# Sixteen weight sums of a two-layer decoder step, moved from the second half's attention to the first half's shared keys and heads

## The chip, the cores and the metric

The kernel runs on one core of a Trainium2 chip. The metric is the device time of one execution in microseconds (us), from the runs of one program on the chip; lower is better. All tensors are fp32. A product of two fp32 matrices is made of three TensorE products of split operands (high times high, high times low, low times high), so that each weight tile is loaded, rounded into a high part by ScalarE, and its rest taken by VectorE, before TensorE can use it.

## The reference, cut to what matters

The reference is one step of a two-layer decoder for a prompt of 1024 tokens and 8 sample tokens, model width 1024, feed-forward width 2816 (22 blocks of 128).

```python
# layer 0: h = h + norm(mixer_a(norm(h)));  h = h + norm(swiglu(norm(h), w_gu[0], w_down[0]))
sb_k, sb_v = split(rmsnorm(h, g_kv) @ w_kv)          # shared keys and values, once, after layer 0
# layer 1: mixer_b(norm(h)) = [stick_breaking(q_s, sb_k, sb_v), mem_attend(q_m, mem_k, mem_v)] @ w_o[1]
#          h = h + norm(mix);  h = h + norm(swiglu(norm(h), w_gu[1], w_down[1]))
def swiglu(h, w_gu, w_down):
    gate, up = split(h @ w_gu, 2)
    return (silu(gate) * up) @ w_down
```

The sample tokens attend, in layer 1, over 256 past tokens each, whose keys and values lie in pages (`cache_sb_k`, `cache_sb_v`) that `page_table` names, and over 256 memory tokens each (`cache_mem_k`, `cache_mem_v`).

## The kernel before, in words

**Two halves.** The prompt is worked in two halves of 512 tokens, g = 0 and g = 1; the 8 sample tokens ride with g = 1, which so has 520 columns. Everything is held transposed: feature blocks of 128 on the partitions, tokens along the free dimension. Each half goes through layer 0 and layer 1. Generators (`a0`, `a1`, `b0`, `b1` for the mixers, `f0`, `f1`, `fw` for the feed-forward, `o0`, `o1` for the output projections) yield after small pieces, and `weave` interleaves several generators in given proportions. The instruction order of every engine is fixed when the program is built; what `weave` decides is the order written into each engine's queue.

**The body's order around the change** (lines 1512 to 1547): `f0` ends layer 0 of g = 0. Then come `o1.mm` (output projection of layer 0 for g = 1, line 400, whose copy out of PSUM is line 388 in `evac_raw`) beside `f0.finish` and `normed`; `kv_proj(0)` (line 1251: four key heads through `proj`, whose copy to SBUF is line 1271, and the values through `rows_proj`, matmul line 1018); `normed` for layer 1; `b0.heads()` (eight heads of queries through `heads2`, copy line 1202) beside `o1.finish()`. `o1.finish` begins with `residual` (line 355): it loads four tiles `ht` of the input (line 362), turns them on TensorE (line 370) and adds them to the projection on VectorE (lines 371 and 373). Then comes `b0`'s attention beside `f1`'s first two parts, `fw`'s three parts, and the same sequence for the other half, up to `b1`'s attention (line 1542). That last stage holds `b1.sb` and `b1.mem` for the prompt, `b1.sb_sample` and `b1.mem_sample` for the sample tokens, and four parts of `f0`'s feed-forward.

**Weights.** `split_w` (line 194) loads 256 KB of weights as 512-byte rows into one of 5 raw tiles `w` (line 199, SyncE's queue), ScalarE rounds it (line 204), VectorE takes the rest (line 205), into one of 5 tiles `ws`. `rows_proj` does the same with rows of 2 KB (lines 1010 to 1013). All plain loads and stores are issued by SyncE (SP) in one order.

**The sample's attention.** `sample_scores` (line 893) loads for each of the 8 tokens its keys `c` (pages through GpSimd, line 953; memory through SP, line 941) and its query, spread over the partitions, `b<-qd` (line 911), multiplies them on VectorE (line 912) and reduces them. `sample_pv` (line 918) loads the values, multiplies (line 924) and adds (line 925) on VectorE, and collects them in a matmul `ns` (line 926). The tiles `c` come from a pool of 4. VectorE takes these instructions in the order of its queue, between the weight rests and the prompt's attention.

**Weight sums.** Part of the feed-forward for g = 1 (`gate_up_w`, line 471) uses seven products of half size instead of eight, and needs sums of blocks of `w_gu` for that. `weight_sums(l, parts)` (line 538) makes them by DMA alone, in DRAM tiles `wsum`: for each part eight steps, four that copy (line 556) and four that add into the destination (line 554).

```python
mark = nc.gpsimd.tensor_copy(small([P, 1], tag="mk", bufs=1), now[0])   # line 551
with tc.issue_after(mark.ins):
    if add: nc.gpsimd.dma_start(d, a, accum_op=ALU.add)                 # line 554
    else:   nc.gpsimd.dma_start(d, a, max_dma_last_dim=4 * w)           # line 556
```

The mark is a copy of one column of `now[0]`, the tile that the other work wrote last when the step was recorded; so GpSimd (POOL) reaches the step's DMA only once that tile is written. Steps of one part depend on each other (step 3 adds into what step 1 copied, step 4 into what step 2 copied, and steps 5 to 8 follow each other), and POOL waits for the landing of the step before. The parts of the feed-forward are 5, 5, 4, 4 and 4 blocks; a step of the first two parts has 1280 KB, of the others 1024 KB.

`ws` is the generator of layer 1's forty steps (parts 0 to 4). Before, steps 1 to 16 (parts 0 and 1) run beside `b0`'s attention, steps 17 to 24 (part 2) beside `fw`, and steps 25 to 40 (parts 3 and 4) beside `b1`'s attention. All are read in the last stage, `f1 = ffn_w(1, ...)`.

Of the kernel before, what the change touches and what calls it, by code (L numbers as in the profile page):

```python
# [23 lines left out]
def tile_decoder(  # L24
# [8 lines left out]
    ND = D // P  # L33
# [57 lines left out]
    def N():  # L91
        return npool.tile([P, WID], F32, tag="n", name=nm("n"))
# [14 lines left out]
    def X(g):  # L107
        return xpool.tile([P, 2, NG[g]], F32R, tag=f"x{g}", name=nm("x"))
# [42 lines left out]
    def gcol(l, i, k):  # L151
        o = (l * 4 + i) * ND + k
        return par[:, o : o + 1]
# [13 lines left out]
    def drain(*gens):  # L167
        for g_ in gens:
            for _ in g_:
                pass  # L170

    def chain(*gens):
        for g_ in gens:
            yield from g_

    def weave(*streams):

        live = [[0, n, g_] for g_, n in streams]
        while live:
            cur = min(live, key=lambda e: e[0] / e[1])  # L180
            cur[0] += 1
            try:
                next(cur[2])
            except StopIteration:
                live.remove(cur)
# [5 lines left out]
    def sv(ap, g):  # L191
        return ap[:, :G] if g == 0 else ap.rearrange("p (a n) -> p a n", a=2)
# [31 lines left out]
    def split_to(dst, src):  # L224
        nc.scalar.copy(dst[0], src)  # L225
        nc.vector.tensor_sub(dst[1], src, dst[0].bitcast(F32))  # L226
# [25 lines left out]
    def sq_acc(acc, src, k, n):  # L252
        if k == 0:
            nc.scalar.activation(acc[:, :n], src, AF.Square)
        else:
            t = N()
            nc.scalar.activation(t[:, :n], src, AF.Square)  # L257
            nc.vector.tensor_add(acc[:, :n], acc[:, :n], t[:, :n])  # L258

    def normed(g, R, rstd, gc, out, keep=False):  # L260
        n = NG[g]
        for k in range(ND):
            t = N() if keep else R[k]
            nc.vector.scalar_tensor_tensor(t[:, :n], R[k][:, :n], gc(k), rstd[:, :n], op0=ALU.mult, op1=ALU.mult)
            x = X(g)
            split_to((x[:, 0, :n], x[:, 1, :n]), t[:, :n])
            out.append(x)
            yield
# [43 lines left out]
        nc.vector.tensor_scalar(xt, xt, ss[:n], None, op0=ALU.mult)  # L312

    made = [None]

    def start(g, out):
        if g:
# [66 lines left out]
    def evac_raw(g, R, ps, m, acc, first, last):  # L384
        n = NG[g]
        dst = sv(R[m], g)
        if first:
            nc.scalar.copy(dst, pv(ps, g))
        else:
            nc.vector.tensor_add(dst, dst, pv(ps, g))  # L390
        if last:
            sq_acc(acc, R[m][:, :n], m, n)

    class out_proj:

# [130 lines left out]
        now[0] = mt[:, 0, 0:1].bitcast(F32)  # L526
        return mt

    now = [None]
    act = [None]  # L530
    sums = {}

# [5 lines left out]
    def weight_sums(l, parts):  # L538

        for i in parts:  # L540
            f0, nf = PARTS[i]
            w = nf * P
            s1, s2, s3, s4 = (tc.dram_tile([512, w], F32, name=nm("wsum")) for _ in range(4))
            sums.setdefault(l, {})[i] = (s1, s2, s3, s4)
            a11, a12 = (w_gu[l][r : r + 512, f0 * P : f0 * P + w] for r in (0, 512))
            a21, a22 = (w_gu[l][r : r + 512, DFF + f0 * P : DFF + f0 * P + w] for r in (0, 512))
            for d, a, add in (
                (s3, a11, False), (s1, a21, False), (s3, a21, True), (s1, a22, True),
                (s2, s3, False), (s2, a22, True), (s4, s2, False), (s4, a12, True),
            ):  # L550
                mark = nc.gpsimd.tensor_copy(small([P, 1], tag="mk", bufs=1), now[0])
                with tc.issue_after(mark.ins):
                    if add:
                        nc.gpsimd.dma_start(d, a, accum_op=ALU.add)
                    else:
                        nc.gpsimd.dma_start(d, a, max_dma_last_dim=4 * w)
                yield
# [122 lines left out]
    class ffn:  # L680
# [4 lines left out]
        def part(self, pi):  # L685
            g, l = self.g, self.l
            n = NG[g]
            f0, nf = PARTS[pi]
            last = pi == len(PARTS) - 1
            mids = []  # L690
            for j in range(nf):
                pg = proj(g, w_gu[l], 0, ND, (f0 + j) * P, self.xt)
                sg = silu(None, pg, g)
                pu = proj(g, w_gu[l], 0, ND, DFF + (f0 + j) * P, self.xt)
                nc.vector.tensor_mul(sv(sg, g), sv(sg, g), pv(pu, g))  # L695
                mt = M(F32R)
                split_to((mt[:, 0, :n], mt[:, 1, :n]), sg[:, :n])
                mids.append(mt)
                now[0] = mt[:, 0, 0:1].bitcast(F32)
                yield  # L700
            if pi == 0:
                self.R = R_one()
            if last:
                self.acc = small([P, WID], tag="st", bufs=3)
            for m in range(ND):
                ps = proj(g, w_down[l], f0, nf, m * P, mids)
                evac_raw(g, self.R, ps, m, self.acc, pi == 0, last)
                now[0] = self.R[m][:, 0:1]
                if m % 2:
                    yield  # L710

# [539 lines left out]
    def kv_proj(g, xt):  # L1251
        ks = small([P, 2, H, NB], tag="ks", bufs=1) if g else None
        for j, (out, scr) in enumerate(((sbk_prompt, ksc), (sbv_prompt, vsc))):
            if j and not g:
                rows = [C(), C()]
                yield from rows_proj(w_kv, H * P, xt, rows)
                for i in range(2):
                    t0 = 2 * i * P
                    nc.sync.dma_start(
                        out[0, t0 : t0 + 2 * P].rearrange("(c p) h d -> p c (h d)", p=P), rows[i]  # L1260
                    )
                    for h in range(H):
                        nc.sync.dma_start(
                            scr[h][:, g, t0 : t0 + 2 * P].rearrange("p (c d) -> p c d", c=2),
                            rows[i][:, :, h * P : (h + 1) * P],
                        )
                continue
            for h in range(H):
                ps = proj(g, w_kv, 0, ND, (j * H + h) * P, xt)
                t = T()  # L1270
                nc.scalar.copy(sv(t, g), pv(ps, g))
                if g:
                    nc.vector.tensor_copy(ks[:, j, h, :], t[:, G : G + NB])
                pt = S()
                for c in range(CH):
                    nc.tensor.transpose(pt[:, c * P : (c + 1) * P], t[:, c * P : (c + 1) * P], ident)
                tok = T()
                nc.vector.tensor_copy(tok[:, :G], pt)
                nc.sync.dma_start(
                    out[0, g * G : (g + 1) * G, h, :].rearrange("(c p) d -> p c d", p=P),  # L1280
                    tok[:, :G].rearrange("p (c d) -> p c d", d=P),
                )
                nc.sync.dma_start(scr[h][:, g, :], t[:, :G] if j == 0 else tok[:, :G])
                yield
        if g:
            for j, dst in enumerate((sbk_sample, sbv_sample)):
                pt = S()
                for h in range(H):
                    nc.tensor.transpose(pt[:NB, h * P : (h + 1) * P], ks[:, j, h, :], ident)
                t = T()  # L1290
                nc.vector.tensor_copy(t[:NB, :512], pt[:NB, :])
                nc.sync.dma_start(dst.rearrange("b o h d -> (b o) (h d)"), t[:NB, :512])
            yield
# [139 lines left out]
    with tc.issue_after(made[0].ins):  # L1433
# [16 lines left out]
        for lv in range(7):  # L1450
            m = 1 << lv
# [48 lines left out]
    a1 = mixer_a(1, x1)  # L1500
# [6 lines left out]
    f0 = ffn(0, 0, o0.x)  # L1507
# [5 lines left out]
    xk0, xb0 = [], []  # L1513
    o1 = out_proj(1, 0, M)
    drain(o1.mm(a1.xo, 0, 1))
    weave((f0.finish(True), 9), (o1.mm(a1.xo, 1, 5), 4))
    weave((normed(0, f0.R, f0.r, gkvcol, xk0, True), 8), (o1.mm(a1.xo, 5, 7), 2))
    drain(kv_proj(0, xk0))
    weave((normed(0, f0.R, f0.r, lambda k: gcol(1, 0, k), xb0), 8), (o1.mm(a1.xo, 7, ND), 1))
    b0 = mixer_b(0, xb0)  # L1520
    weave((b0.heads(), 8), (o1.finish(), 17))
    b0.open()
    f1 = ffn(1, 0, o1.x)
    ws = weight_sums(1, range(5))
    weave((chain(b0.sb(), b0.mem()), 25), (chain(f1.part(0), f1.part(1)), 18), (islice(ws, 16), 17))
    set_banks(True)
    fw = ffn_w(0, o1.x, (5, 6, 5), 2, False, f1.R)
# [13 lines left out]
    f0 = ffn(0, 1, o0.x)  # L1541
    weave(
        (chain(b1.sb(), b1.mem()), 45), (chain(b1.sb_sample(), b1.mem_sample()), 39),
        (chain(f0.part(0), f0.part(1), f0.part(2), f0.part(3)), 34), (ws, 17),
    )
    o1 = out_proj(1, 1, A, True)
    drain(o1.mm(b1.xo))
# [37 lines left out]
```

## Time and profile before

| | before |
|---|---|
| median of 3 runs | 2512.58 us (2512.22 to 2516.48) |
| the profiled execution's own time | 2513.78 us |
| its span, first to last instruction | 2511.9 us |
| mean granted TensorE clock | 0.995 |
| TensorE matmul busy | 2467.7 us |
| VectorE busy | 1609.2 us |
| ScalarE busy | 1197.4 us |
| GpSimd busy | 119.6 us |

The profile is of one execution. Engines are named PE (TensorE matmul), PEld (its weight load), DVE (VectorE), ACT (ScalarE), POOL (GpSimd) and SP (SyncE, which issues DMAs). A row of the timeline or of the chain begins with its start in us from the span's start and its length in us; in square brackets stands how long the engine was idle before it and who ended that. A row of the stretches view gives for one stretch of time its length, each engine's busy time with the number of instructions, the granted TensorE clock (1.00 is full speed), the busy share of the 16 DMA engines and the rate in GB/s. In the DMA view, q1 is the queue that SP fills and q0 the one that POOL fills; the last column of a queue's row is the share of the 16 engines' time that its packets took, and the last number of an issue row is the median time from issue to landing.

### The profile page before, as it was taken

What the parts mean: (1) busy time and instruction counts of PE and PEld (TensorE: products, weight loads), DVE (VectorE), ACT (ScalarE), POOL (GpSimd) and SP (SyncE); (2) the same over time, 40 slices, a digit from 0 to 9 for tenths busy, and PEclk for the clock granted to TensorE, in tenths of its full rate; (3) what the DMA queues carried; (4) which work ended last, traced back from release to release, by engine and by line L of the source; (5) the groups of instructions that cost most, each with busy time, mean ns of one, the idle gap of its engine ahead of it and who ended that gap; (6) DMA issues with size and microseconds to landing.
All of it is one profiled execution on the core that took longest, in us unless ns stands there. A gap on an engine that the chain in (4) does not pass through costs nothing.

```text
span 2511.9 us, 40889 instructions
## 1 busy us (share of the span) xinstructions
PE 2467.7 (98%) x15455; PEld 2160.5 (86%) x15455; DVE 1609.2 (64%) x2900; ACT 1197.4 (48%) x2289; POOL 119.6 (5%) x187
## 2 busy tenths in 40 slices
PE   8999999999999999999999999999999999999998
PEld 6888888877877898999999989876677798999998
DVE  5766556654766576665655676776687538845666
ACT  5437543243433454554434554554454335554445
POOL 1000000000000000010100100021000000000000
PEclk9999999999999999999999999999999999999999
DMA  5355656554743447476767746575456643464552
GB/s 189 116 158 126 162 174 164 130 145 144 195 122 101 130 138 219 148 181 163 187 177 194 221 139 191 167 193 143 135 167 169 167 123 118 134 186 140 150 151 73
DMA packets 521550, 391.24 MB, mean 156 GB/s; under 512 B 19973, under 2 KB 459858, under 8 KB 521354
## 3 DMA queue, kind: packets, MB, share of 16 engines
q1 hardware_dynamic: 493194, 308.94, 41.4%
q0 software_dynamic: 28160, 79.70, 13.4%
q8 instruction: 121, 1.98, 0.3%
q14 instruction: 75, 0.61, 0.1%
HBM read 358.76 MB, written 101.11 MB: 183 GB/s over the span
## 4 chain that ended last, share of the span: by engine, by line
PE 90%; DVE 4%; DMA 3%; ACT 1%; issue 1%; SPq 0%; POOL 0%; DVEq 0%; ACTq 0%
PE mm L218 53%; PE q L499 11%; PE q L631 7%; PE q L453 2%; PE s L1150 2%; PE mm L1018 2%; DMA b<-qd 1%; PE s L1343 1%; PE s L885 1%; PE s L854 1%; PE mm L803 1%; PE mm L830 1%; PE s L1314 1%; PE q L663 1%; PE ns L926 1%
## 5 line engine op out<-in xcount | busy, mean ns | idle before, releaser
L218 PE MATMUL mm<-x,ws 128*128 128x512 f32 (+1 forms) x6624 | 1216.0, 340 | 2.4 <-DVE t L235 1.5
L218 PEld LDWEIGHTS mm<-x,ws 128*128 128x128 f32 x6624 | 1013.6, 189 | 155.5 <-issue 17.4
L204 ACT CAST ws<-w 128x512 fp32r<-128x512 f32 (+1 forms) x672 | 395.1, 589 | 616.8 <-PE mm L218 468.3
L205 DVE TENSOR_TENSOR ws<-w,ws 128x512 fp32r<-128x512 f32 (+1 forms) x672 | 435.1, 651 | 259.7 <-ACT ws L204 247.5
L218 PE MATMUL mm<-m,ws 128*128 128x512 f32 (+1 forms) x1536 | 329.3, 367 | 0.0
L218 PEld LDWEIGHTS mm<-m,ws 128*128 128x128 f32 x1536 | 255.1, 189 | 51.3 <-issue 1.9
L631 PE MATMUL q<-m,ws 128*128 128x260 f32 x1440 | 175.7, 283 | 0.0
L631 PEld LDWEIGHTS q<-m,ws 128*128 128x128 f32 x1440 | 173.4, 188 | 0.9 <-DVE t L522 0.5
L490 DVE TENSOR_TENSOR ws<-w,ws 128x512 fp32r<-128x512 f32 x164 | 112.4, 691 | 79.7 <-ACT ws L489 77.1
L489 ACT CAST ws<-w 128x512 fp32r<-128x512 f32 x164 | 101.4, 621 | 98.8 <-PE q L631 33.1
L499 PE MATMUL q<-x,ws 128*128 128x260 f32 x1008 | 134.3, 282 | 0.0
L499 PEld LDWEIGHTS q<-x,ws 128*128 128x128 f32 x1008 | 126.4, 188 | 0.0
L499 PE MATMUL q<-y,ws 128*128 128x260 f32 x912 | 119.3, 283 | 0.1
L499 PEld LDWEIGHTS q<-y,ws 128*128 128x128 f32 x912 | 113.5, 189 | 0.3 <-ACT q L506 0.3
L235 DVE TENSOR_SCALAR t<-mm 128x512 f32<-128x512 f32 (+1 forms) x70 | 48.4, 691 | 57.6 <-PE mm L218 57.3
L695 DVE TENSOR_TENSOR t<-t,mm 128x512 f32<-128x512 f32 (+1 forms) x54 | 37.2, 689 | 60.0 <-PE mm L218 59.9
L390 DVE TENSOR_TENSOR r<-r,mm 128x512 f32<-128x512 f32 (+1 forms) x72 | 49.4, 686 | 39.9 <-PE mm L218 39.0
L239 DVE TENSOR_TENSOR t<-t,t 128x512 f32<-128x512 f32 (+1 forms) x54 | 37.4, 693 | 55.4 <-ACT t L238 55.4
L226 DVE TENSOR_TENSOR m<-t,m 128x512 fp32r<-128x512 f32 (+1 forms) x88 | 61.0, 693 | 6.8 <-ACT m L225 5.3
L225 ACT CAST m<-t 128x512 fp32r<-128x512 f32 (+1 forms) x88 | 54.9, 624 | 21.7 <-DVE t L695 13.0
L453 PE MATMUL q<-x,ws 128*128 128x260 f32 x480 | 61.0, 288 | 3.7 <-DVE r L390 2.2
L258 DVE TENSOR_TENSOR st<-st,n 128x512 f32<-128x512 f32 (+1 forms) x91 | 62.4, 694 | 2.9 <-ACT n L257 1.5
(342 smaller groups left out, 2869.1 us busy)
## 6 DMA issues: line engine op xcount, KB each, us to landing
w<-in_w_gu SPq DMA_DIRECT2D x310, 256.0 KB, 3.2
w<-in_w_down SPq DMA_DIRECT2D x160, 256.0 KB, 2.9
wsum<-in_w_gu POOLq DMA_DIRECT2D x36, 1024.0 KB, 9.6
w<-wsum SPq DMA_DIRECT2D x94, 256.0 KB, 3.3
w<-in_w_in_a SPq DMA_DIRECT2D x80, 256.0 KB, 3.2
w<-in_w_o SPq DMA_DIRECT2D x64, 256.0 KB, 2.8
wsum<-in_w_gu POOLq DMA_DIRECT2D x12, 1280.0 KB, 10.5
wsum<-wsum POOLq DMA_DIRECT2D x12, 1024.0 KB, 6.6
```

Of the source, the lines that this page charges most:

```text
L204: nc.scalar.copy(ws[:, 0, :n, :], raw[:, :n, :])
L205: nc.vector.tensor_sub(ws[:, 1, :n, :], raw[:, :n, :], ws[:, 0, :n, :].bitcast(F32))
L218: nc.tensor.matmul(ps[:, a, : PW[g]], wt, xt[k][:, xi, o : o + PW[g]], start=(k == 0 and wi == 0), stop=(k == nk - 1 and wi == 2),)
L225: nc.scalar.copy(dst[0], src)
L226: nc.vector.tensor_sub(dst[1], src, dst[0].bitcast(F32))
L258: nc.vector.tensor_add(acc[:, :n], acc[:, :n], t[:, :n])
L453: ins = nc.tensor.matmul(pp[a][:, :h], wt, xt[k][:, xi, a * h : (a + 1) * h], start=(k == 0 and wi == 0), stop=(k == ND - 1 and wi == 2),)
L489: nc.scalar.copy(w[:, 0, :], src)
L490: nc.vector.tensor_sub(w[:, 1, :], src, w[:, 0, :].bitcast(F32))
L499: nc.tensor.matmul(ps[:, :h], w[:, wj, k * P : (k + 1) * P], x[:, xi, :], start=(first and k == 0 and wi == 0), stop=(k == 3 and wi == 2), ...
L631: nc.tensor.matmul(pp[a][:, :h], wt, mids[k][:, xi, a * h : (a + 1) * h], start=(k == 0 and wi == 0), stop=(k == nf - 1 and wi == 2),)
L1018: nc.tensor.matmul(pb[i][:, a, :], xt[k][:, xi, c * P : (c + 1) * P], ws[:, s, :], start=(k == 0 and wi == 0), stop=(k == ND - 1 and wi == 2),
```

## The change

The sixteen steps that ran beside `b1`'s attention are no longer there. All forty steps of `ws` begin earlier by sixteen: parts 0 and 1 are now made beside the first half's norm, shared keys and heads (3 + 5 + 2 + 6 steps), parts 2 and 3 beside `b0`'s attention, part 4 beside `fw`. For the marks, `now[0]` is now also set by `evac_raw` (so by the output projections too) and by `kv_proj`. The instructions of PE, DVE, ACT and SP stand in the same order as before, one for one; only POOL's order and the tiles that marks read are changed. One side effect lies in the first half: four of layer 0's sums, beside `o0.finish`, now have marks that read `o0`'s last projection tile instead of a tile of `a1`'s heads.

```diff
@@ evac_raw
         if last:
             sq_acc(acc, R[m][:, :n], m, n)
+        now[0] = R[m][:, 0:1]
@@ ffn.part
                 evac_raw(g, self.R, ps, m, self.acc, pi == 0, last)
-                now[0] = self.R[m][:, 0:1]
@@ kv_proj
                 nc.sync.dma_start(scr[h][:, g, :], t[:, :G] if j == 0 else tok[:, :G])
+                now[0] = t[:, 0:1]
                 yield
@@ body, first half
-    weave((normed(0, f0.R, f0.r, gkvcol, xk0, True), 8), (o1.mm(a1.xo, 5, 7), 2))
-    drain(kv_proj(0, xk0))
-    weave((normed(0, f0.R, f0.r, lambda k: gcol(1, 0, k), xb0), 8), (o1.mm(a1.xo, 7, ND), 1))
+    ws = weight_sums(1, range(5))
+    weave((normed(0, f0.R, f0.r, gkvcol, xk0, True), 8), (o1.mm(a1.xo, 5, 7), 2), (islice(ws, 3), 3))
+    weave((kv_proj(0, xk0), 8), (islice(ws, 5), 5))
+    weave((normed(0, f0.R, f0.r, lambda k: gcol(1, 0, k), xb0), 8), (o1.mm(a1.xo, 7, ND), 1), (islice(ws, 2), 2))
     b0 = mixer_b(0, xb0)
-    weave((b0.heads(), 8), (o1.finish(), 17))
+    weave((b0.heads(), 8), (o1.finish(), 17), (islice(ws, 6), 6))
     b0.open()
     f1 = ffn(1, 0, o1.x)
-    ws = weight_sums(1, range(5))
     weave((chain(b0.sb(), b0.mem()), 25), (chain(f1.part(0), f1.part(1)), 18), (islice(ws, 16), 17))
@@ body, second half
         (chain(b1.sb(), b1.mem()), 45), (chain(b1.sb_sample(), b1.mem_sample()), 39),
-        (chain(f0.part(0), f0.part(1), f0.part(2), f0.part(3)), 34), (ws, 17),
+        (chain(f0.part(0), f0.part(1), f0.part(2), f0.part(3)), 34),
     )
```

More of the change, by code (lines that the diff above doesn't have):

```diff
@@ L314, in tile_decoder @@
     made = [None]
+    now = [None]
     def start(g, out):
@@ L527, in gate_up_w @@
         return mt
-    now = [None]
     act = [None]
```

## The prediction

> **What bounds the kernel now.** I read the page's part 1, then the queues, then the chain that ended last.
>
> ```profile
> span 2511.9 us, 40889 instructions
> ...
> PE 2467.7 (98%) x15455; PEld 2160.5 (86%) x15455; DVE 1609.2 (64%) x2900; ACT 1197.4 (48%) x2289; POOL 119.6 (5%) x187
> ...
> PE 90%; DVE 4%; DMA 3%; ACT 1%; issue 1%; SPq 0%; POOL 0%; DVEq 0%; ACTq 0%
> ```
>
> TensorE is busy for all but 44.2 us of the span, and the change touches no instruction of it. So the change can win only idle time of PE, or time at a lowered clock, and can lose only by making new idle time. I therefore asked the stretches view where PE idles now, and found it in the stage that loses the sums, `b1`'s attention.
>
> ```profile
> 1600.00:2010.00 410.00, 392.24 (x1762) 296.07 (x1762) 284.69 (x444) 188.88 (x362) 45.09 (x56) 0.98 0.58 162
> ...
> 1680.00:1800.00 120.00, 107.05 (x462) 78.34 (x463) 77.46 (x121) 54.98 (x102) 17.71 (x20) 0.94 0.52 143
> ...
> 1880.00:1960.00 80.00, 75.59 (x350) 58.45 (x349) 56.22 (x95) 34.56 (x79) 5.26 (x8) 1.00 0.62 165
> ```
>
> PE idles 17.8 us in the stage's 410, of which 13.0 and 4.4 lie in the two shorter stretches. In the first of these the granted clock is 0.94, which over 120 us is 7.2 us of full-rate time.
>
> Next, what PE waits for there: the chain and the timelines around 1745, where the longest gap is.
>
> ```profile
> 1745.46 1.14 POOL L554 DMA_DIRECT2D wsum<-in_w_gu  x1
> 1746.90 1.05 POOL L953 DMA_INDIRECT c<-in_cache_sb_v,pidx  x1 [0.31 <-issue]
> ```
>
> ```profile
> 1746.90 9.42 DMA c<-in_cache_sb_v,pidx
> ...
> 1756.42 1.24 DVE c L924
> ```
>
> ```profile
> 1762.69 1.09 PE L1338 MATMUL s<-ident,b 128*128 128x128 f32 x4 [4.47 <-DVE b L1301]
> ```
>
> A sum is issued 1.4 us ahead of a page of values on the same queue; the page lands after 9.42 us; VectorE stands at line 924 for it, and with it the prompt's attention and the weight rests that come later in its order; PE then idles 4.47 us. The second stretch has the same form: a query load of 10.32 us beside a sum.
>
> ```profile
> 1906.59 10.32 DMA b<-qd
> ```
>
> ```profile
> DVE c L912 <- DMA b<-qd: 13.8, 9, 3.2
> ...
> DVE c L924 <- DMA c<-in_cache_sb_v,pidx: 12.0, 2, 8.1
> ```
>
> ```profile
> b<-qd SPq DMA_DIRECT2D x24, 256.0 KB, 4.4
> ...
> c<-in_cache_sb_v,pidx POOLq DMA_INDIRECT x16, 4.6
> ```
>
> The usual landing is 4.4 and 4.6 us. VectorE loses 13.8 and 12.0 us to these two loads in the stage; 8.1 of the 12.0 is the wait shown above.
>
> **What the removal gives.** The upper end: all 17.4 us of the two stretches, and of the 7.2 us of lost clock the 6 or so (an estimate) in which PE had work: 23.4. The lower end: only the two longest loads come back to their usual time, 9.42 to 4.6 and 10.32 to 4.4, which is 10.7 us less wait on VectorE and no clock: 11. I take **20**, near the upper end, because the stage's other stretches, with the same loads but shorter waits, idle only 0.4 us together. What is late next is the prompt's attention chain from VectorE to ScalarE, with waits of 1 to 2 us that PE covers with feed-forward matmuls.
>
> **What the addition costs.** The instructions: 16 marks and 16 DMA issues on POOL either way. What matters is the 16 engines' time. The same sixteen sums (parts 0 and 1) run today between 1040 and 1250; the DMA view of that stretch has POOL's queue by itself:
>
> ```profile
> q0 software_dynamic: 6400, 20.97, 43.0%
> ```
>
> 43.0% of 210 us is **90.3 us** of all 16 engines. The stage that receives them, from the projection's sixth column block to the last head (918 to 1040), has SP's own traffic:
>
> ```profile
> q1 hardware_dynamic: 26048, 21.01, 56.0%
> ```
>
> 56.0% of 122 us is **68.3 us**. Together 158.6 us of transfers in 122 us: **36.6 too much**. The marks let the last two sums (a copy and an add, some 11 of the 90.3, estimated by their sizes and landings) start only after the sixth and seventh head, and nothing in the stage reads them; they can end behind it. So about 26 us remain that must come out of SP's loads, unless these have as much slack.
>
> Where it hurts shows in when the traffic falls:
>
> ```profile
> 918.00:970.00 52.00, 52.00 (x256) 42.57 (x254) 34.47 (x55) 23.98 (x42) 0.00 (x0) 1.00 0.42 126
> 970.00:986.00 16.00, 16.00 (x93) 13.37 (x92) 7.39 (x12) 6.35 (x12) 0.00 (x0) 1.00 1.01 321
> 986.00:1040.00 54.00, 53.98 (x299) 45.47 (x298) 41.39 (x74) 29.75 (x52) 0.00 (x0) 1.00 0.57 174
> ```
>
> ```profile
> 976.46 1.88 SPq L362 DMA_DIRECT2D ht<-in_x_prompt  x4
> ```
>
> ```profile
> 983.53 0.67 PE L370 MATMUL ns<-ident,ht 128*128 128x128 f32 x3
> ```
>
> ```profile
>   DMA ht<-in_x_prompt: 0.2, 1
> ```
>
> From 970 to 986 the engines are full (1.01) without any sum: the values' stores, then the four `ht` tiles that `residual` turns on PE. PE reaches line 370 at 983.53 and already waits for `ht` (the 0.2 us in the row of that line). There is no slack at all. PE takes its queue in order, so heads' matmuls behind line 370 can't fill in. By then POOL has issued the eight sums of part 0 (45.2) and, the moment the last column block is copied out, the first two of part 1 (some 7):
>
> ```profile
> 975.46 0.59 ACT L388 COPY m<-mm 128x520 f32<-128x520 f32 x1 [2.25 <-PE mm L218]
> ```
>
> So 45.2 + 7, and SP's 0.42 x 52 + 1.01 x 16 = 38.0, make 90 us of work for the 68 between 918 and 986: **`ht` about 22 us late**. How the engines share decides; the trace has one dense run of sums, 300 to 316:
>
> ```profile
> q0 software_dynamic: 1227, 3.95, 90.7%
> q1 hardware_dynamic: 930, 0.46, 12.8%
> ...
> w<-in_w_o SPq DMA_DIRECT2D x5, 256.0 KB, 13.5
> ```
>
> ```profile
> 300.00:316.00 16.00, 16.00 (x71) 12.98 (x70) 5.25 (x8) 6.14 (x12) 1.13 (x2) 1.00 1.04 276
> ```
>
> POOL's queue had 90.7% and SP's 12.8% while a weight load took 13.5 us. PE did not idle there (16.00 of 16.00), since ten tiles of weights, five raw and five split, stand ahead of it; ahead of `ht` stands nothing. So the sums go first and SP's loads wait. I take 22 for `ht`, 3 for the other late loads up to 1040 (they are the rest of the 26), and 3 for the half-rate clock that follows such gaps (four drops cost the 7.2 above, so 1.8 each): **28**. The ends: 8, if SP's loads get an equal share and only the full stretch slips by half; 40, if all 36.6 and two drops show.
>
> ```profile
> wsum<-in_w_gu POOLq DMA_DIRECT2D x12, 1280.0 KB, 10.5
> ```
>
> ```profile
> 1408.73 1.23 POOL L953 DMA_INDIRECT c<-in_cache_sb_k,pidx  x1 [25.64 <-PE q L499]
> ```
>
> The added waits themselves I put at nothing (0 to 3). Behind a mark on POOL stand only marks and sums, as the first page load is at 1408. Tiles that a mark reads are held until it ran: the key heads' `t`, of 3 buffers, for which the tokens' copy at line 1278 waits; and the last projection tile, which line 371 rewrites in `residual`. A mark runs right after its tile unless POOL still stands at an earlier sum's landing, 10.5 us as a rule; if that cover goes, it adds to a stall that the loads make anyway.
>
> The first half's four sums move from 297.6 to 304.6 to after `o0`'s last copy:
>
> ```profile
> L388 ACT COPY m<-mm x8: 586/587/588, 299.1 to 337.9; 128x512 f32<-128x512 f32 x8
> ```
>
> ```profile
> 297.62 0.65 POOL L556 DMA_DIRECT2D wsum<-wsum  x1
> ...
> 304.60 1.05 POOL L554 DMA_DIRECT2D wsum<-in_w_gu  x1 [4.52 <-DMA wsum<-wsum]
> ```
>
> ```profile
> 333.03 2.40 SPq L362 DMA_DIRECT2D ht<-in_x_prompt  x4
> ```
>
> They begin at about 338.5 then, when the four `ht` loads issued from 333 to 335.4 are almost in. I take 0 (0 to 4). The sums beside `b0`'s attention shrink from 1280 to 1024 KB a step: nothing to 2 gained, since PE idles little there.
>
> **The Trainium skill weighed.** The Trainium skill, "DMA: Bandwidth & Descriptors", section "Queues, rings and completion order", says that each DMA engine takes turns between the queues it has work for, a packet at a time. By it neither queue would starve and the cost would be nearer 12 than 28, the first rival below. The dense run above (90.7 against 12.8) speaks against equal turns by time, though not against turns by packet, as a sum's packets are longer.
>
> **The sum.** 28 lost less 20 won: 8 us slower. On the profiled execution's 2513.8 us (span 2511.9 and 1.9 around it) that is 2521.8; the median of the runs shown stands 1.2 lower, so **2521 us**.
>
> **The rivals.**
> - *Even sharing* (faster). If SP's queue keeps half of the engines whenever it has work, the 16 us of full traffic at 970 slip by about 8 and weights by nothing; with one clock drop and some late loads the cost is 12, against 20 won: 8 faster, 2504.6. It decides at a cost of 20, that is, `ht` less than some 15 us late. For it: between 1040 and 1250, where the same sums run spread out, weight loads land in 4.7 us. Against it: the 12.8%. Chance 0.28.
>
> ```profile
> w<-in_w_gu SPq DMA_DIRECT2D x35, 256.0 KB, 4.7
> ```
>
> - *The sample stage keeps its waits.* The query loads are issued just ahead of their use, so even 4.4 us could leave VectorE waiting; 11 won, 28 lost: 2529.5. For it: `b<-qd` made nine waits, most of them short. Against it: the longest of them, shown above, has a sum beside it. Chance 0.12.
> - *Both equal.* The stall is 20 and so is the gain: within 2 us of 2512.6. Chance 0.08.
> - That the change doesn't move the work is excluded by POOL's order: it has no sum among the page loads of values any more.
>
> **How the numbers follow.** The forecast has 0.52, with a range of its own of 2518 to 2536. Across the cases: 12 to 15 faster with a cheap slip and the full gain (8 against 23.4), to 40 lost against 15 won (25 slower). The range 2497 to 2537 leaves out some 2 in 10. 0.2% (5 us) is about what a measurement of this kernel can tell from no change: faster 0.28, same 0.14, slower 0.58 (the forecast's own tail below 5 us is in the 0.14).
>
> **What would show it.** Right: in the changed profile PE has a gap of 10 us or more at line 370 near 985 that a DMA of `ht` ends, the stretch 918 to 1040 has a DMA share near 1, and the sample stage idles under 4 us at clock 1.00. Wrong: no gap at line 370 (then the sharing was even, and the kernel is faster), or page and query loads that still take 8 to 10 us with no sum in flight.

## The result, and the profile after

| | before | after |
|---|---|---|
| median of 4 runs each | 2513.65 us (2512.22 to 2516.48) | **2528.52 us** (2525.74 to 2533.61) |
| ratio, 95% interval | | **1.006** (1.0041 to 1.0079) |
| profiled execution, its span | 2513.78, 2511.9 us | 2525.74, 2523.9 us |

The changed kernel is 0.6% slower. The profiled execution of after is the fastest of its four, so the spans differ by 12.0 us where the medians differ by 14.9. One of the baseline's later executions, in the set of E9 to E12, was slow (6009.52 us); no ratio uses it, and it moves that set's median by 0.3 us only. Page of after, parts 1 and 4:

```profile
span 2523.9 us, 40867 instructions
...
PE 2467.2 (98%) x15455; PEld 2159.3 (86%) x15455; DVE 1609.5 (64%) x2900; ACT 1197.5 (47%) x2289; POOL 117.3 (5%) x187
...
PE 90%; DVE 3%; DMA 3%; ACT 2%; issue 1%; SPq 0%; POOL 0%; DVEq 0%; ACTq 0%; POOLq 0%
```

The page looks the same as before's: the work of every engine is unchanged, and 12 us of waiting do not show in shares of 2500. The stretches view of after shows what moved (columns as before):

```profile
918.00:1040.00 122.00, 93.91 (x429) 74.15 (x429) 57.98 (x97) 40.12 (x70) 12.55 (x22) 0.89 1.02 279
1040.00:1250.00 210.00, 208.65 (x1543) 194.78 (x1541) 125.12 (x232) 110.42 (x218) 19.53 (x34) 1.00 0.64 162
1600.00:2010.00 410.00, 404.67 (x1930) 312.08 (x1928) 299.33 (x470) 202.67 (x385) 25.80 (x24) 1.00 0.44 131
1680.00:1800.00 120.00, 115.12 (x532) 86.56 (x530) 91.60 (x143) 62.65 (x116) 20.00 (x18) 0.99 0.44 133
```

In 918 to 1040 PE, busy for all of it before, is busy for 93.91 of 122 us, at a clock of 0.89, with the DMA engines full (1.02). In the second half's attention PE's idle time fell from 17.8 to 5.3 us and the clock is back at 1.00. The change did both things that it was expected to do, and the price was the larger.

PE's instructions stand in one order in both kernels, so the start of the same instruction in both traces gives the account: after stands 3.2 us *earlier* at 918; 31.5 later from 1030 on (the stage costs **34.7**); 28.85 later by 1400 (2.6 came back, most of it at 1253); and 11.95 later from 1960 to the end (the second half's attention gave **16.9**). −3.2 + 34.7 − 2.6 − 16.9 = 12.0. The 3.2 is scatter of single executions, as is shown below; without it the sum is 15.2, near the medians' 14.9. What PE waited for between 900 and 1060 in after, in us, times, longest:

```profile
PE ns L371 <- DMA ht<-in_x_prompt: 14.1, 3, 9.4
PE s L1276 <- ACT t L1271: 8.2, 1, 8.2
PE ns L247 <- DVE st L258: 5.4, 1, 5.4
```

These are 27.7 us of gaps; the other 7.0 of the 34.7 are matmuls at the lower clock that follows the gaps. The wait for `ht` (line 370 before, 371 after) was forecast. The third is one of the "other late loads" of the forecast: ScalarE stood 5.39 us for a weight until 1031.85, and the squares that line 258 adds up stood behind it. The second wait was not forecast. It is the key heads' transposes, in the timeline of after:

```profile
930.96 0.19 POOL L552 COPY mk<-t 128x1 f32<-128x1 f32 x1 [6.76 <-ACT t L1271]
...
933.08 0.53 POOL L552 COPY mk<-t 128x1 f32<-128x1 f32 x1 [0.46 <-ACT t L1271]
```

```profile
939.01 0.69 DVE L1278 COPY t<-s 128x512 f32<-128x512 f32 x1 [5.45 <-DMA ksc<-t]
...
946.35 0.58 ACT L1271 COPY t<-mm 128x512 f32<-128x512 f32 x1 [10.60 <-DMA out_sbk_prompt<-t]
...
946.99 1.11 PE L1276 MATMUL s<-ident,t 128*128 128x128 f32 x4 [8.23 <-ACT t L1271]
```

A key head takes two of the three `t` buffers: the copy of the head and its turned copy `tok`. Both are stored to DRAM by SP (into `ksc` and `out_sbk_prompt`), and a buffer is free only when its store has landed. The stores were slow beside four sums, VectorE waited 5.45 us for one, ScalarE 10.60 for the next, and PE for ScalarE. The marks had run at 931 and 933 and held nothing. Before, the same copy stood 2.11 us behind PE itself:

```profile
941.03 0.59 ACT L1271 COPY t<-mm 128x512 f32<-128x512 f32 x1 [2.11 <-PE mm L218]
```

How the engines were shared from 975 to 995, in the DMA view of after, when SP alone had 100.3% before:

```profile
q0 software_dynamic: 980, 3.54, 71.8%
q1 hardware_dynamic: 2676, 2.09, 32.9%
```

### The profile page after: what moved, and what is told of

Read it like the earlier page. It is cut to its first block, busy times and chain, and to the rows that moved or that the text cites. A ratio compares the mean times of both kernels' runs of the same rounds, so it can differ in the third digit from the quotient of the medians.

```text
span 2523.9 us, 40867 instructions
## 1 busy us (share of the span) xinstructions
PE 2467.2 (98%) x15455; PEld 2159.3 (86%) x15455; DVE 1609.5 (64%) x2900; ACT 1197.5 (47%) x2289; POOL 117.3 (5%) x187
## 4 chain that ended last, share of the span: by engine, by line
PE 90%; DVE 3%; DMA 3%; ACT 2%; issue 1%; SPq 0%; POOL 0%; DVEq 0%; ACTq 0%; POOLq 0%
PE mm L218 53%; PE q L501 11%; PE q L632 6%; PE s L1150 2%; PE mm L1018 2%; PE q L455 2%; PE s L885 1%; PE s L1344 1%; DMA w<-in_w_in_b 1%; PE s L854 1%; PE s L1315 1%; PE mm L803 1%; PE mm L830 1%; PE q L664 1%; PE ns L926 1%
## 5 line engine op out<-in xcount | busy, mean ns | idle before, releaser
L218 PEld LDWEIGHTS mm<-x,ws 128*128 128x128 f32 x6624 | 1015.7, 189 | 154.2 <-issue 14.1
L225 ACT CAST m<-t 128x512 fp32r<-128x512 f32 (+1 forms) x88 | 54.9, 624 | 14.1 <-DVE t L696 4.9
```

The source lines that it names most:

```text
L218: nc.tensor.matmul(ps[:, a, : PW[g]], wt, xt[k][:, xi, o : o + PW[g]], start=(k == 0 and wi == 0), stop=(k == nk - 1 and wi == 2),)
```

## The experiments

**Theory**: the loss is transfers of the sums that displace SP's in 918 to 1040, the gain is the same transfers taken from beside the page and query loads, and the two add up. **Rivals**: the marks make the waits; the sample stage keeps its waits; the queues share evenly. The baseline's median was 2511.8, 2513.6 and 2513.3 us in the three sets of runs (E1 to E4, E5 to E8, E9 to E12).

**E1, the changed kernel with marks only in the stage that got the sums.**

```diff
-    ws = weight_sums(1, range(5))
+    ws = weight_sums(1, range(5), (0, 1))    # marks run, the DMAs of parts 0 and 1 are left out
```

> The changed kernel, whose sixteen steps beside the norm, shared keys and heads are marks only: their DMAs are left out, and layer 1's feed-forward of the second half reads plain slices of w_gu where it read the sums of parts 0 and 1 (so these products are of other data). Theory (the loss is the transfers in this stage): no gap of PE over 1 us at the key heads' transposes or at line 371, the stage costs nothing against before, and the time is before less the gain in the second half's attention, some 17 to 20 us less, 2493 to 2498 us. Rival (the marks hold GpSimd and the tiles t, ns): the gap at 947 and at least part of those near 1000 stay, the time is 2515 us or more.

2493.8 us, ratio to before 0.9924 (0.9908 to 0.9941): 18 us faster. The stretches view of this run:

```profile
918.00:1040.00 122.00, 122.00 (x645) 101.53 (x645) 83.32 (x139) 60.24 (x105) 5.50 (x16) 1.00 0.57 173
```

PE is busy for all 122 us with all sixteen marks in place. The loss is the transfers; the marks cost nothing here.

**E2, before with marks only beside the second half's attention.**

```diff
-    ws = weight_sums(1, range(5))
+    ws = weight_sums(1, range(5), (3, 4))    # the DMAs of parts 3 and 4 are left out
```

> The kernel before, whose sixteen steps beside the second half's attention are marks only: their DMAs are left out, and the feed-forward reads plain slices of w_gu in place of the sums of parts 3 and 4. Theory (the gain is the transfers beside page and query loads): 17 to 20 us faster than before, 2493 to 2498 us, with PE idle under 5 us from 1600 to 2010, clock 1.00 and page loads of 4 to 5 us. Rival (the sample stage keeps its waits, or the marks make them): gain of 11 us or less, 2502 us or more, with line 912 still waiting over 8 us.

2496.4 us, ratio 0.9939 (0.9922 to 0.9955): 15.4 us faster, a little under the theory's 17 to 20 and far from the rival's 11 or less. PE's idle time from 1600 to 2010 is 6.0 us, where the theory had said under 5:

```profile
1600.00:2010.00 410.00, 404.01 (x1880) 308.21 (x1879) 290.25 (x455) 193.38 (x372) 31.75 (x40) 1.00 0.42 124
```

**E3, before with sixteen sums more.** All of before's sums stay; parts 0 and 1 are made once more where the change puts them, with its marks.

```diff
+    xw = weight_sums(1, range(2), True)      # into tiles that nothing reads
+    # beside normed, kv_proj, normed, heads: islice(xw, 3), (xw, 5), (xw, 2), (xw, 6)
```

> The kernel before with all its sums in place, and sixteen further sums (parts 0 and 1 once more, into tiles that nothing reads) beside norm, shared keys and heads, with the marks of the changed kernel. Theory (the cost of the addition stands alone, the two sides add up): 29 to 36 us slower than before, 2542 to 2550 us, with the gaps near 947, 1000 and 1034 as in the changed kernel. Rival (even sharing, the cost is nearer 12 and the rest of the changed kernel's loss is elsewhere): 2522 to 2528 us.

2549.8 us, ratio 1.0152 (1.0135 to 1.0169): **38 us slower**. The loss alone is a little above the theory's end; 38 less the 15 to 18 of E2 and E1 makes 20 to 23, where the change cost 14.9. The remainder is within the intervals (each of some 4 to 5 us either way). In the trace the stage costs 38.1 us in E3 and 34.7 in after, and E3 keeps the large sums beside the first half's attention, where after got 2.6 back.

**E4, the same forty sums elsewhere.**

```diff
-    drain(f0.part(4))
+    weave((f0.part(4), 8), (islice(ws, 4), 4))
...
-    weave((chain(b0.sb(), b0.mem()), 25), (chain(f1.part(0), f1.part(1)), 18), (islice(ws, 16), 17))
+    weave((chain(b0.sb(), b0.mem()), 25), (chain(f1.part(0), f1.part(1)), 18), (islice(ws, 20), 21))
-    weave((o1.finish(), 17), (f0.part(4), 8))
+    weave((o1.finish(), 17), (f0.part(4), 8), (ws, 9))
```

> All forty sums made, none beside norm, shared keys and heads and none beside the second half's attention: four steps beside the last part of f0 in the first half, twenty beside b0's attention (sixteen before), eight beside fw, and the last eight beside the last part of f0 in the second half. Theory (both costs are of the place, not of the sums): 2494 to 2501 us, 13 to 19 us faster than before. Rival (wherever the sums stand they displace loads that PE needs): a new stall in one of the stretches that got more of them, 2508 us or more.

**2493.11 us**, ratio 0.9922 (0.9906 to 0.9939), as fast as E1, which makes sixteen sums fewer. The first half's attention takes four sums more without loss (DMA share 0.76 of 210 us, PE idle 1.4, as before):

```profile
1040.00:1250.00 210.00, 208.63 (x1614) 198.15 (x1613) 131.39 (x266) 108.29 (x223) 26.36 (x40) 1.00 0.76 188
```

None stand beside the norm, the shared keys and the heads, and none beside the second half's attention. Both costs belong to the places, not to the sums. What stayed open was how the loss comes about: by the excess of transfers, or by single loads.

**E5 and E8, eight and four further sums** in place of E3's sixteen, at the stage's start.

```diff
-    xw = weight_sums(1, range(2), True)
+    xw = weight_sums(1, range(1), True)      # E5: (xw, 3) beside normed, (xw, 5) beside kv_proj
                                              # E8: (xw, 4) beside normed, none behind
```

> The kernel before with eight further sums (part 0 once more, into tiles that nothing reads) beside the norm and the shared keys, half of the sixteen that cost 38 us. Theory (what the engines can't do in time is late): 45.2 us of sums and 38 of SP's transfers for the 68 us up to 986 leave 15 too much, and with the stall at the key heads' transposes the cost is 13 to 20 us, 2525 to 2532 us. Rival (only the sums in flight beside the values' stores and ht matter): the eight are done by about 985, so under 8 us, 2520 us or less.

> The kernel before with four further sums only (two copies and two adds of part 0 once more, 22.6 us of the engines by the arithmetic of the forecast), all beside the norm of the shared keys. Theory (the excess decides): 22.6 and 38 are 60.6 us of transfers for the 68 up to 986, so nothing is late at ht, and at most the key heads' stores are: 0 to 6 us, 2512 to 2518 us. Rival (any sum in this stage displaces loads that PE needs, by its share): a quarter of 38 or more, 2521 us or above.

E5: 2533.96 us, 1.008 (1.0063 to 1.0097), 20 slower, the upper end of the theory's 13 to 20. E8: 2524.74 us, 1.0046 (1.0029 to 1.0063), **11 slower**. The theory missed E8: by its sum, four sums had room before `ht` and should have cost at most 6. They cost a quarter of the sixteen's price and more, and PE's waits from 880 to 1100 in E8 say where:

```profile
PE s L1276 <- ACT t L1271: 8.2, 1, 8.2
PE s L1339 <- DVE b L1302: 0.7, 1, 0.7
```

All of it is the key heads' `t`; at `ht` nothing is late. The forecast's sum was made up to the wrong deadline: the first transfers that PE can't do without are the key heads' stores near 941, not `ht` at 983.

**E9, E8 with the turned copies in other buffers.**

```diff
-                tok = T()
+                tok = T() if g else B()          # seven b tiles, idle in this stage
```

> The kernel with four further sums beside the norm (11 us slower than before), its key heads' turned copies tok placed in the seven b tiles, idle in this stage, in place of the three t tiles. Theory (the 11 us are one stall: ScalarE at line 1271 can't write t while the slow stores of t and tok hold its three buffers): no gap at line 1276, cost 0 to 3 us against before, 2512 to 2517 us. Rival (the values' weights, line 1010, are late by themselves and stop PE a few us later): 6 us or more, 2519 us or above.

2513.9 us, ratio 0.9999 (0.999 to 1.0009): **the four sums cost nothing**.

```profile
918.00:970.00 52.00, 52.00 (x256) 42.62 (x255) 34.57 (x55) 23.23 (x39) 5.59 (x6) 1.00 0.87 238
```

With the engines 0.87 busy PE has no gap. So the first deadline is one of buffers, and four sums fit into the stage as the sum of transfers had it, once that is eased.

**E10, the changed kernel with that edit; E7, with `ht` earlier; E12, with both.**

```diff
+    early = input_tiles(1)                       # E7, E12: the ht loads, written ahead of normed
-    weave((b0.heads(), 8), (o1.finish(), 17), (islice(ws, 6), 6))
+    weave((b0.heads(), 8), (o1.finish(early), 17), (islice(ws, 6), 6))
```

> The changed kernel with the same edit: tok in b tiles. Theory (36.6 us of excess come out anyway, at the next thing PE waits for): the gap at line 1276 goes, that at line 371 grows by most of it, and the time falls by 4 us at most, 2524 us or more. Rival (each stall has its own price): 8 to 12 us less than the changed kernel, 2516 to 2520 us.

> The changed kernel, with the four ht loads issued by SP before the norm of the shared keys, ahead of all sixteen sums, instead of behind the values' stores. Theory (most of the second stall is that nothing stands ahead of ht, while weights have tiles ahead): the gap at line 371 is gone, the excess falls on weights with some 13 us of cover, and the stage loses 15 to 20 in place of 34.7: 2506 to 2514 us. Rival (the excess of transfers stays, and stops PE at the next load instead): 2522 us or more.

> The changed kernel with both edits: ht loaded ahead of the sums, and tok in b tiles. Theory (excess of transfers over time): with both nearest deadlines eased, the loss moves to stores and weights behind them, and at least 20 us of 34.7 stay: 2513 us or more. Rival (the loss is these two deadlines): under 10 us stays, 2505 us or less.

E10: 2524.67 us (1.0047, 1.0032 to 1.0063), 4 us less than the changed kernel. E7: 2525.75 us (1.0051, 1.0034 to 1.0068), 3 less. E12: 2520.91 us (1.0028, 1.0017 to 1.0039), 8 less. The intervals of E10 and E7 overlap that of the changed kernel (1.0041 to 1.0079), so their times alone show no gain; E12's does not. In E7 and E12 the edit reached less far than meant: `ht` waited for its buffers and was issued at 981.35 and 973.97, behind the first of the values' ten stores. The waits for it still fell from 14.1 us to 4.2 and 3.9, and the time by less. In E10 PE's waits from 880 to 1100 begin with

```profile
PE ns L371 <- DMA ht<-in_x_prompt: 18.7, 3, 13.5
```

so that 4.6 of the 8.2 us saved at line 1276 are waited for at `ht` instead (18.7 against 14.1), and in E12 with

```profile
PE ns L378 <- DVE m L381: 14.0, 1, 14.0
PE ns L247 <- DVE st L258: 4.1, 1, 4.1
PE ns L378 <- DMA ht<-in_x_prompt: 3.9, 2, 2.9
```

(line 378 is the changed kernel's 371). Behind the first row stands a weight load, in the timeline of E12:

```profile
1010.71 0.62 ACT L204 CAST ws<-w 128x512 fp32r<-128x512 f32 x1 [23.22 <-DMA w<-in_w_in_b]
...
1012.42 0.70 DVE L258 TENSOR_TENSOR st<-st,n 128x520 f32<-128x520 f32 x1 [14.24 <-ACT n L257]
```

ScalarE stood 23.22 us at the rounding of a weight, and the squares `n` of the residual, which were ready, stood behind it in its queue; VectorE waited for those and PE for VectorE. By the account of equal instructions the stage costs 30.4, 30.1 and 29.9 us in E10, E7 and E12 against 34.7. So some 30 us stay whichever deadline is eased, as the excess of transfers would have it: the next load is late by it. E7's theory had failed on this point: weights have tiles of cover, but ScalarE's queue has other work behind them.

**E11, the four further sums behind `ht`.**

```diff
-    weave((b0.heads(), 8), (o1.finish(), 17))
+    weave((b0.heads(), 8), (o1.finish(), 17), (chain([None] * 2, islice(xw, 4)), 6))
```

> The kernel before with the same four further sums, beside the second half of the heads, behind ht, where SP's transfers take 0.57 of the engines and leave 23 us of 54 free. Theory (a sum costs nothing where the engines have room before PE's next deadline): 0 to 4 us slower than before, 2512 to 2518 us. Rival (a sum costs about 0.45 us for each us of engines that it takes, wherever in this stage): 9 us or more, 2522 us or above.

2526.75 us, ratio 1.0046 (1.0029 to 1.0062): 12 slower, the rival's number. PE's waits from 880 to 1100:

```profile
PE s L1315 <- DMA a<-ksc: 9.6, 1, 9.6
PE s L1339 <- DVE b L1302: 0.7, 1, 0.7
```

Another load with nothing ahead of it: `a<-ksc`, the first keys of the attention that follows, the second of which SP began to issue at 1027.35 (before: 1022.91) and took 8.08 us to issue (before: 0.49). The stage's average share of 0.57 says nothing about such a load.

**E6, E3's sums in pieces of 512 bytes.**

```diff
-                        nc.gpsimd.dma_start(d, a, accum_op=ALU.add)
+                        for r in (0, 256):
+                            nc.gpsimd.dma_start(d[r : r + 256], a[r : r + 256], accum_op=ALU.add, max_dma_last_dim=512)
                    # the copies likewise: max_dma_last_dim=512 in place of 4 * w
```

> The kernel before with the same sixteen further sums, made in pieces of 512 bytes in place of 2048 bytes and more (each add issued as two DMAs of half the rows). Theory (the sums' engine time decides, and short pieces only add to it): the loss is 38 us or more, 2550 us or above. Rival (the engines take turns by packet, so that long packets crowd out SP's 512-byte rows and short ones would not): ht and the weights land sooner, and the loss is under 25 us, below 2537 us.

2570.73 us, ratio 1.0232 (1.0215 to 1.0249): 57 slower, the theory's number, but not by its reason. PE's longest waits:

```profile
PE ns L371 <- DVE m L374: 24.2, 1, 24.2
PE s L1281 <- ACT t L1276: 8.4, 1, 8.4
PE ns L371 <- DMA ht<-in_x_prompt: 4.2, 3, 2.7
```

and behind the first, in the timeline:

```profile
1033.98 0.76 DVE L372 SCALAR_TENSOR_TENSOR m<-m,par,st 128x520 f32<-128x520 f32 x1 [24.48 <-POOL mk L552]
```

Here a mark made the wait: POOL, slower with the short pieces, had not yet read the projection tile that VectorE was to rewrite. And SP's loads did land sooner: PE waits 4.2 us for `ht` here and 17.0 in E3. The DMA view from 978 to 990, E3 and then E6:

```profile
q0 software_dynamic: 528, 1.31, 67.8%
q1 hardware_dynamic: 1358, 1.01, 27.4%
```

```profile
q1 hardware_dynamic: 3468, 2.48, 73.6%
q0 software_dynamic: 1296, 0.66, 45.7%
```

In both, SP's queue passed 2.6 to 2.7 pieces for each of POOL's (1358 to 528, 3468 to 1296; the view calls them packets). With long pieces that was 27.4% of the engines, with short ones 73.6%. The Trainium skill, "DMA: Bandwidth & Descriptors", section "Queues, rings and completion order", has each engine take turns between its queues by packets of several descriptors, not by time. These rows agree: the share of time follows the length of the pieces. They don't settle it, since POOL also issued its sums more slowly in E6.

## Why the prediction was right, step by step

- **The side and the sum held**: 8 slower forecast, 2521 us; measured 14.9, 2528.52, inside the forecast's own range. Two terms were mis-sized, both too kindly: the cost 28 for 34.7, the gain 20 for 16.9; 2.6 came back at a place that had been put at nothing.
- **What the removal gives, 20.** Measured 16.9 in the two profiles, 18 in E1, 15 in E2. Page loads of values land in 4.1 us again. The rest, 5.3 us of idle time against "under 4", is mainly PE's wait at the attention's line 1339 for VectorE, 3.2 us at its longest in after. It also stands in E1 and E2 (2.9 and 3.7) without a sum near it. The forecast named that chain as late next, and wrongly held it covered.
- **What the addition costs, 28.** The arithmetic held: 26 to 36.6 us of excess, and 30 to 38 lost in E3, after, E7, E10 and E12. The step that failed is where it falls. "Where it hurts shows in when the traffic falls" looked only at 970 to 986. PE was 24.9 us late at its last wait for `ht`, close to the 22, but 10.0 of them had already been lost at line 1276 (8.2 of gap and the clock behind it); only the rest is `ht`'s. E8 and E9 show that first stall by itself: 11 us with four sums, none with other buffers. In E10, where it is gone, PE is 21 us late at the same wait: the sum up to `ht` was sound, and an earlier deadline was left out. The other late loads, put at 3, made a gap of 5.4.
- **The half-rate clock, 3.** Measured 7.0 (34.7 less 27.7 of gaps). The forecast counted drops of 1.8, four in the 7.2 us; the trace's records of the clock show three there, at half rate for 6.83, 3.41 and 3.41 us. In the stretch from 1000 to 1040 the granted clock was 0.81.
- **The added waits, nothing.** Right for this change (E1). Its warning, that tiles read by a mark are held, was right in E6, where one such wait was 24.5 us. It named the key heads' `t` as held by the marks. In the change it was held by its stores; in E6 VectorE did wait 11.47 and 14.49 us for marks on it.
- **The marks moved in the first half, nothing (0 to 4).** The traces show a small cost. In nine of the twelve kernels with the moved marks PE waits 0.6 to 2.1 us at `residual` near 361, for VectorE, which stands 2.7 to 4.3 us at `c<-in_state_hgrn` (line 1093), a load that now runs beside the moved sums. Before and E2, which have the old marks, show neither wait. In after's own trace VectorE waits 1.50 us there and PE does not wait. After was 3.2 us early before 880 all the same; with the same first half E1 and E4 were 0.9 and 1.2 late, and E2, which has before's, 3.0 early. That is scatter of single executions.
- **The smaller sums beside the first half's attention, nothing to 2.** 2.6 came back. Before's gap of 2.21 us near 1253 is gone in after, E1, E4, E7, E10 and E12, and stands at 1.7 to 3.1 in the seven other kernels, which keep before's sums there. That it is the size of the sums is not shown: E4 has twelve of the large ones in this stretch and no gap.
- **The rivals.** Even sharing: SP's queue had 32.9% where it had used 100.3%, so the sums went mostly first. The sample stage that keeps its waits: excluded by E1 and E2.
- **What would show it.** The gap at line 371 came, as three (9.4, 2.1 and 2.7) and at 1000 instead of 985, behind the stall that wasn't seen; the DMA share is 1.02. The sample stage idles 5.3 us where under 4 was asked, at clock 1.00.

Open: how much of the 34.7 a kernel could win back with all sixteen sums in this stage; E12 is the nearest, with 7.6 us over before. Not tried: `ht` in buffers of its own, loaded before the first sum.

## What to carry to other kernels

Before moving background transfers, find in the receiving stage each transfer that PE needs with no buffer of slack in front, stores that free a buffer among them, and add up the traffic to the *first* of these; the average share of the engines doesn't tell. If the whole stage has more transfers than time, easing one deadline hands most of the wait to the next (some 30 of 34.7 us here). Put such work where loads have tiles of cover to spare: the same forty sums made this kernel 18.7 us faster in E4 and 14.9 slower in the change.

## What the runs showed of the hardware

- Issuing itself took SP longer while sums were in flight. The four `ht` issues took 1.88 us before, and in after:

```profile
987.98 6.01 SPq L363 DMA_DIRECT2D ht<-in_x_prompt  x4
```

  In E11 one issue took 8.08 us in place of 0.49. The DMA engines were full around `ht` in both kernels (1.01 from 970 to 986 before, 1.02 from 986 to 1040 after), so their share alone does not decide it; what does, no run here shows. SP issues in one order, so a late issue delays the stores behind it as well as the loads.
- The same bytes cost more of the engines in short pieces: from 918 to 1040 POOL's queue moved 17.04 MB in 57.1% of 122 us in E3 (4.1 us of all 16 engines a MB), and 11.79 MB in 52.2% in E6 (5.4 us a MB).
